# Nine expert units instead of ten: two experts' worth of places given to four in one of the units loaded ahead

## The chip, the core and the metric

The kernel runs on one core of one Trainium2 chip. The metric is device time in microseconds of one execution, taken as the median of a few runs. TensorE multiplies, VectorE, ScalarE and GpSimd (POOL in the profile) do the rest, SyncE (SP) issues loads, and 16 DMA engines move the bytes. The profile calls TensorE PE, VectorE DVE and ScalarE ACT.

## The reference

The reference is one decoder block for 256 tokens of width 1024 in float32. A forgetting attention and a gated delta rule run side by side and are merged. Then comes a mixture of 32 experts, each of which has three weights of 1 MiB (1024x256, 1024x256, 256x1024). Last come a per-layer input embedding, gated by a 1024x1024 weight, and a normalization. The change lies in the mixture, which is this:

```python
gl = t @ w_group + b_group                       # 4 groups
g_sel = argmax(gl);  p_sel = softmax(gl)[g_sel]
el = (t @ w_router + b_router)[group g_sel]      # 8 experts of the group
top_p, top_i = top_k(softmax(el), 2);  top_p /= sum(top_p)
gate = one_hot(g_sel) x (p_sel * top_p at top_i) # 256 x 32, two entries a token
for e in range(32):
    hid = silu(t @ w_gate[e]) * (t @ w_up[e])
    out = out + gate[:, e:e+1] * (hid @ w_down[e])
...
x = x + sigmoid(rmsnorm(x) @ w_ple_gate) * (p @ w_ple_proj)
```

Each token chooses two of 32 experts, so an expert gets 16 tokens on average. With the reference's inputs, the experts 0 to 5 get 17, 31, 12, 12, 14 and 21 tokens. The others, in descending order, get 36, 23, 23, 21, 21, 20, 18, 17, 17, 17, 16, 16, 16, 15, 15, 15, 13, 13, 11, 11, 11, 11, 9, 8, 6 and 6.

## The kernel before

The first 250 us are the two mixing branches, the output projection and the routing. While they run, SP already loads the weights of the experts 0 to 5 (`NSTAY = 6`), which are taken whatever the routing is. The other 26 are ordered by their number of tokens on the chip (`order_experts`). POOL then loads their weights with indirect transfers, whose row indices come from that order. "Expert 6" and so on below mean places in this order.

A **unit** is a set of experts that are computed together, and `UNITS` lists them. A unit always has 128 rows. A unit of two experts gives each 64 places for tokens, one of four gives each 32. Before the change there are ten units: four pairs (experts 0 to 7) and six fours (8 to 31). The last units are the **late** ones, from `UE = NU - 3` on, thus units 7, 8 and 9. Their experts have few tokens, so that only the first 16 of each 32 places (`FEW`) count. If an expert has more tokens than places, the flag that `order_experts` computes is set. A branch (`crowded`, `overflow`) then runs a loop over all experts and windows of 64 tokens. When the flag is not set, every engine jumps over it.

What happens for unit i:

- `group(i // 2)` gathers the token features of two units at once: VectorE writes 0/1 choices into the tile `G` (`one_hot`), TensorE multiplies the tokens (`xx`, high and low parts) by them into `ga`, and ScalarE copies the result into `XT`. `XT` has three halves that rotate, and `half(i)` says which half of a group a unit uses.
- `gate_up` multiplies `XT` by each expert's gate and up weights. Each expert of the unit writes its own 64 or 32 rows of the result tiles `gate` and `up`.
- `silu` and `hidden` form the hidden values, turn them (`hidT`) and multiply by the down weights into `dn` (and `ga` for the second half of a late unit).
- `parts` spreads an early unit's result over the tokens: `C` is the turned choice, and the products go into the four tiles `sum`. A late unit's result goes through `late_parts`, `late_spread` (into the finished rows) and `z_late`. The latter multiplies its turned rows by the final gate weight and spreads the product into the final gate's sums.

The final gate's product for the tokens as the early units leave them is made ahead, in `z_early`: 64 products of 128x512 with `w_ple_gate`, which start after the gate of the first late unit (`after("gate", UE + 1)`). `early_features` makes their operand once all early units are in. `last_down`, `z_last` and what they call finish the last unit in three pieces.

The weights go through a ring of places of 1 MiB: 20 in the expert stage, one more late (`xx`). `experts(u)` queues for each unit its gate weights, then the up weights, then the down weights. The down weights of the late units and of the one ahead of them go in halves or quarters. The extra embedding's weight `wpp` is queued ahead of expert 6. The four tiles of the final gate weight, `wpg`, are queued ahead of the gate weights of the unit that `WPG = (7, "g")` names. `Ring.pump` issues the next load as soon as a place is free, strictly in the order of the queue. Eight loads can be under way on POOL's queue, since each waits for the one eight issues earlier.

A planner (`Plan`) with rough costs merges the generators into one fixed order of instructions for each engine when the kernel is built. At run time each engine takes its instructions in that order. Every operation goes through one helper, so that the profile shows most of them at line 77, and tiles tell more than lines. An f32 product is two records in the profile and one row in the order.

Of the kernel before, what the change touches and what calls it, by code (L numbers as in the profile page):

```python
# [10 lines left out]
AF = mybir.ActivationFunctionType  # L11
OP = mybir.AluOpType
# [7 lines left out]
E = 32  # L20
CAP = 64


NSTAY, NWIDE = 6, 8
UNITS = [list(range(e, e + 2)) for e in range(0, NWIDE, 2)] + [list(range(e, e + 4)) for e in range(NWIDE, E, 4)]
NU = len(UNITS)

WPG = (7, "g")

UE, UL = NU - 3, NU - 1  # L30

FEW = 16
FIRST = UNITS[UE - 1][0]
# [64 lines left out]
class Plan:  # L98
# [25 lines left out]
    def after(self, name, n=1):  # L124
        return lambda: 0.0 if n <= 0 else self.told[name][n - 1] if len(self.told.get(name, ())) >= n else None
# [166 lines left out]
def hybrid_block(tc, x, p_t, w_in, w_o_fox, w_o_delta, w_out, w_gate, w_up, w_down, w_ple_gate,  # L292
                 w_ple_proj, g_final, keep_in, mix_in, out, dbg=None):
    nc = tc.nc
    plan = Plan(nc)
    V, S, P, G = plan.V, plan.S, plan.P, plan.G
# [80 lines left out]
    def K(name):  # L377
        a, b = KEEP[name]
        return kp[:, a:b]

    ident = K("ident")
    ones = keep.tile([128, 128], F32, name="ones")
# [846 lines left out]
    def last_tile():  # L1229
        for n in range(2):  # L1230
            yield after("sq1", n + 1)
            turned(1, n)
            yield
        logits(1, 0)
        yield
        yield after("sel")
        rank(0)
        logits(1, 1)
        yield
        yield from ffn_norm(1)  # L1240
        yield
        yield after("parts", 2)

        d = td[:, 0, :].rearrange("p (e s) -> p e s", s=CAP)
        for e in range(4):
            S.activation(d[:, e, :], K("slots"), AF.Square, scale=-1.0, bias=rk[:, 0, e:e + 1])
        S.activation(g0[:, 0].rearrange("p a (e s) -> p (a e) s", s=CAP), d, AF.Relu, scale=-1.0, bias=ones[:, 0:1])
        pr[1] = ps_t("mm")
        P.matmul(pr[1][:, 0:E], ones, sel[:, 0, :], start=True, stop=False)
        busy(6)  # L1250
        for k in range(4):
            gather(0, k)
        yield from route(1)
        rank(1)
        for k in range(4, 8):
            gather(0, k)
        busy(0)
        places(1)
        yield
# [71 lines left out]
    def half(i):  # L1331

        return (i % 2) ^ (i // 2 % 3 == 1)
# [64 lines left out]
    def order_experts():  # L1398
        yield after("sel", 2)
        pt = ps_t("dn")  # L1400
        for t in range(2):
            P.matmul(pt[0:32, 0:32], ones[:, 0:32], sel[:, t], start=t == 0, stop=t == 1)
        for t in range(2):
            P.matmul(pt[0:32, 32:33], sel[:, t], ones[:, 0:1], start=t == 0, stop=t == 1)
        yield
        keys, key, at = so[:, 0:32], so[:, 32:33], so[:, 33:34]
        V.scalar_tensor_tensor(key, pt[0:32, 32:33], 64.0, K("base")[0:32, 32:33], op0=OP.mult, op1=OP.add)
        V.scalar_tensor_tensor(keys, pt[0:32, 0:32], 64.0, K("base")[0:32, 0:32], op0=OP.mult, op1=OP.add)
        V.tensor_scalar(keys, keys, key, None, op0=OP.is_gt)
        V.tensor_reduce(at, keys, axis=AX.X, op=OP.add)  # L1410
        V.tensor_scalar(perm, K("places")[0:32, 0:32], at, None, op0=OP.is_equal)
        yield
        pt = ps_t("dn")
        P.matmul(pt[:, 0:32], K("places")[0:32, 32:33].to_broadcast([32, 128]), perm, start=True, stop=True)
        yield
        V.tensor_scalar(idx, pt[:, 0:32], K("places")[:, 33:34], None, op0=OP.add)
        tell("idx")
        V.tensor_scalar(rowf, pt[:, E - late:E], K("places")[:, 33:34], None, op0=OP.add)
        ring.index, ring.pieces = idx, idp
        ring.pump()  # L1420
        yield
        yield after("gate")
        yield from permute(rk, rkp, K("w_rt")[0:32, 0:256])
        tell("rkp")
        for (a, b), ix in idp.items():
            V.tensor_scalar(ix, rowf, 4.0 / (b - a), float(a // (b - a)), op0=OP.mult, op1=OP.add)
        yield after("weights")
        r = mo.tile([128, 2, 128], F32, name="hidT").rearrange("p k s -> p (k s)")[0:32]
        yield from permute(gr[:, :, :, 1], grp[:, :, :, 1], r)
        V.tensor_copy(grp[:, :, :, 0], gr[:, :, :, 0])  # L1430
        tell("grp")

        V.tensor_scalar(so[:, 34:35], at, NWIDE - 0.5, 32.0, op0=OP.is_lt, op1=OP.mult)
        V.tensor_scalar(so[:, 35:36], at, UNITS[UE][0] - 0.5, float(FEW - 32), op0=OP.is_gt, op1=OP.mult)
        V.tensor_tensor(so[:, 34:35], so[:, 34:35], so[:, 35:36], op=OP.add)
        yield
        pt = ps_t("sum00")
        P.matmul(pt[:, 0:32], so[:, 34:35].to_broadcast([32, 128]), ident[0:32, 0:32], start=True, stop=True)
        yield
        for t in range(2):  # L1440
            V.scalar_tensor_tensor(rko[:, t], rk[:, t], -32.0, pt[:, 0:32], op0=OP.add, op1=OP.subtract)
        V.tensor_reduce(big[:, 0:1], rko.rearrange("p t e -> p (t e)"), axis=AX.X, op=OP.max)
        yield
        pt = ps_t("sum00")
        P.transpose(pt[0:1, 0:128], big[:, 0:1], ident)
        yield
        V.tensor_reduce(big[0:1, 1:2], pt[0:1, 0:128], axis=AX.X, op=OP.max)
        V.tensor_scalar(flag, big[0:1, 1:2], 1.0, None, op0=OP.is_ge)
        tell("flag")
        yield  # L1450
# [16 lines left out]

    def group(i):

        yield after("rows", 2 * i - 2)  # L1470
        yield after("group", i - 1)
        yield after("G", i)
        g = mo.tile([128, 2, 2, 128], F32R, name="G") if i % 2 else g0
        X = XT[:, (slice(0, 2), slice(0, 3, 2), slice(1, 3))[i % 3]]
        wt = mo.tile([128, 2, 2], F32, name="wt", bufs=2)
        QD[i] = (g, wt)
        if i:
            yield after("rkp")
        for t in range(2) if i else (1,):
            yield after("rk", t + 1)  # L1480
            ranks = rkp if i else rk
            if half(2 * i) or 2 * i < UE <= 2 * i + 1:
                for a in range(2):
                    h = half(2 * i + a)
                    one_hot(g[:, t, h:h + 1], ranks[:, t], UNITS[2 * i + a])
            else:
                one_hot(g[:, t], ranks[:, t], UNITS[2 * i] + UNITS[2 * i + 1])
        tell("G")
        yield after("parts", 2)
        yield after("group", i)  # L1490
        yield after("gu", max(0, 2 * i - 1))
        for k in range(8):
            if i:
                yield turn()
                pt = ps_t("ga")[:, 0:256]
                n = 0
                for t in range(2):
                    for part in (xH, xL):
                        P.matmul(pt, part[:, t, k, :], g[:, t].rearrange("p a s -> p (a s)"), start=n == 0, stop=n == 3)
                        n += 1  # L1500
                plan.add(features_of(i, k, X, pt))
            else:
                gather(1, k)
                if k % 2:
                    for kk in (k - 1, k):
                        plan.add(features_of(i, kk, X, xb[kk // 2][:, kk % 2 * 256:kk % 2 * 256 + 256]))
                if k < 7:
                    continue
            yield
        yield after("grp" if i else "weights")  # L1510
        yield turn()

        pt = ps_t("ga")
        for a in range(2):
            u = UNITS[2 * i + half(2 * i + a)]
            m = 128 // len(u)
            for t in range(2):
                for o, e in enumerate(u):
                    P.matmul(pt[o * m:(o + 1) * m, 2 * a:2 * a + 2], g[:, t, a, o * m:(o + 1) * m].bitcast(F32), (grp if i else gr)[:, t, e, :],
                             start=t == 0, stop=t == 1, skip_group_check=True)  # L1520
        yield
        V.tensor_copy(wt.rearrange("p a b -> p (a b)"), pt[:, 0:4])
        tell("wt")
        tell("ga")
        tell("group")
        yield

    def features_of(i, k, X, pt):
        pt = pt.rearrange("p (a s) -> p a s", a=2)
        if True:  # L1530
            S.activation(X[:, :, k], pt, AF.Copy, scale=K("g_ffn")[:, k:k + 1])
        else:
            V.tensor_scalar(X[:, :, k], pt, K("g_ffn")[:, k:k + 1], None, op0=OP.mult)
        tell(f"X{i}")
        if i:
            tell("ga")
        yield
# [598 lines left out]
        nc.sync.dma_start(out[t * 128:(t + 1) * 128, 0:512], th)  # L2136
        yield

    for i in range(NU // 2):
        plan.add(group(i))  # L2140
    plan.add(add_x2())
    plan.add(order_experts())
# [95 lines left out]
```

## Time and profile before

| | |
|---|---|
| median of 3 runs | 536.14 us (535.42 to 536.36) |
| the profiled execution | 535.39 us, of which its span is 533.4 us |
| mean granted TensorE clock | 0.969 |
| TensorE busy | 499.9 us, 94% of the span |
| VectorE, ScalarE, GpSimd busy | 229.7, 210.4 and 133.9 us |
| moved by DMA | 141.25 MB, 265 GB/s over the span |
| loads issued by POOL (software_dynamic) | 86.01 MB |
| gate products of units 7, 8 and 9 start at | 411.49, 447.96 and 483.38 us |

The span runs from the first to the last instruction, and all times inside it count from its start. A busy TensorE need not be TensorE at its peak. A row of the chain of work says when a piece starts, how long it is, and on which engine and tile. A row of POOL's timeline shows an issue of a load, and in brackets how long POOL stood idle before it and what ended that.

### The profile page before, as it was taken

The page shows a single profiled execution, that of the slowest core. Times are in us where ns is not written, and L with a number is a line of the kernel's source. Part 1 is how long each engine was busy: PE and PEld are TensorE (multiplying, and loading weights), DVE is VectorE, ACT ScalarE, POOL GpSimd, SP SyncE. Part 2 cuts the span into 40 slices and gives each one's busy share as a digit, 9 for nine tenths or more (in the row PEclk, how much of TensorE's full clock was granted, in tenths as well). Part 3 has the DMA queues.
Part 4 walks back from the last instruction along what each step waited for, and adds up shares of the span by engine and source line. Part 5 has one row for each costly group of instructions (what it writes and reads, how often), then busy time and mean ns, then how long its engine had stood idle before and what let it go on. Part 6 is the DMA issues. An engine that isn't in the chain of part 4 may idle for free. (4 is left out here: it accounts for less than half of the span.)

```text
span 533.4 us, 10476 instructions
## 1 busy us (share of the span) xinstructions
PE 499.9 (94%) x4375; PEld 351.0 (66%) x4375; DVE 229.7 (43%) x543; ACT 210.4 (39%) x475; POOL 133.9 (25%) x160
## 2 busy tenths in 40 slices
PE   7999999999999999979999999968986999989993
PEld 7999998899999999868555554423543444433441
DVE  3888689764655659584311111100123011012246
ACT  5576845566734545344231221203244011021144
POOL 5000551200000000061233324316444226425000
PEclk9999999999999999998999999979996999998997
DMA  8845533223098569875979999998999996985002
GB/s 343 347 159 167 192 119 115 67 89 131 7 402 303 170 225 423 314 289 188 358 278 384 367 378 340 373 396 308 412 421 416 421 412 227 421 349 201 1 1 79
DMA packets 25605, 141.25 MB, mean 265 GB/s; under 512 B 2625, under 2 KB 2897, under 8 KB 12626
## 3 DMA queue, kind: packets, MB, share of 16 engines
q0 software_dynamic: 14752, 86.01, 41.3%
q1 hardware_dynamic: 10658, 54.01, 27.0%
q8 instruction: 36, 0.59, 0.4%
q10 hardware_dynamic: 144, 0.52, 0.2%
q14 instruction: 15, 0.12, 0.1%
HBM read 139.46 MB, written 1.05 MB: 263 GB/s over the span
## 5 line engine op out<-in xcount | busy, mean ns | idle before, releaser
L77 PE MATMUL mm<-hH,ra 128*128 128x256 f32 x688 | 127.1, 284 | 0.0
L77 PEld LDWEIGHTS mm<-hH,ra 128*128 128x128 f32 x688 | 105.6, 188 | 1.5 <-issue 0.3
L77 PE MATMUL mm<-hL,ra 128*128 128x256 f32 x344 | 83.8, 281 | 0.5 <-DVE hL L77 0.5
L77 PEld LDWEIGHTS mm<-hL,ra 128*128 128x128 f32 x344 | 64.8, 188 | 1.4 <-DVE hL L77 0.7
L77 DVE TENSOR_TENSOR ra<-ra,ra 128x1024 fp32r<-128x1024 f32 x41 | 50.3, 1231 | 18.2 <-ACT ra L77 18.2
L77 ACT CAST ra<-ra 128x1024 fp32r<-128x1024 f32 x41 | 42.9, 1053 | 27.1 <-PE mm L77 23.2
L77 DVE TENSOR_TENSOR yL<-dn,yH 128x512 fp32r<-128x512 f32 x16 | 11.1, 692 | 71.8 <-ACT yH L77 71.8
L77 ACT ACTIVATE XT<-ga,kp 128x256 f32<-128x256 f32 x32 | 15.1, 473 | 55.3 <-PE ga L77 55.3
L77 POOL CAST xx<-xt 128x1024 fp32r<-128x1024 f32 (+1 forms) x2 | 3.3, 1648 | 126.5 <-ACT td L77 123.8
L77 PE MATMUL gate<-ra,XT 128*32 128x256 f32 (+1 forms) x224 | 34.0, 402 | 0.0
L77 PE MATMUL up<-ra,XT 128*32 128x256 f32 (+1 forms) x240 | 33.0, 393 | 0.0
L77 PE MATMUL ga<-G,xx 128*128 128x256 f32 x128 | 23.0, 303 | 7.7 <-PEq L1710 5.1
L77 PE MATMUL gate<-rb,XT 128*32 128x256 f32 (+1 forms) x176 | 30.2, 397 | 0.0
L77 PEld LDWEIGHTS ga<-G,xx 128*128 128x128 f32 x128 | 18.2, 193 | 16.6 <-issue 10.1
L77 DVE SCALAR_TENSOR_TENSOR kp<-th,wt,up 128x256 f32<-128x256 f32 x10 | 4.8, 480 | 52.8 <-PE up L77 52.8
L77 PE MATMUL dn<-ra,hidT 128*32 128x512 f32 (+2 forms) x88 | 23.1, 578 | 0.3 <-DVE rc L77 0.3
L77 PE MATMUL sum<-ra,xx 128*128 128x512 f32 x48 | 22.9, 599 | 0.0
L77 PEld LDWEIGHTS up<-ra,XT 128*32 128x32 f32 (+1 forms) x240 | 14.5, 120 | 11.2 <-issue 5.5
L77 PEld LDWEIGHTS gate<-ra,XT 128*32 128x32 f32 (+1 forms) x224 | 15.0, 124 | 10.2 <-issue 6.1
L77 ACT COPY hidT<-ga 128x256 f32<-128x256 f32 x10 | 3.7, 372 | 40.9 <-PE ga L77 40.9
L77 ACT CAST yH<-dn 128x512 fp32r<-128x512 f32 x16 | 9.3, 583 | 24.1 <-PE dn L77 14.1
L77 PE MATMUL gate<-rc,XT 128*32 128x256 f32 (+1 forms) x64 | 18.0, 416 | 0.0
(477 smaller groups left out, 1097.5 us busy)
## 6 DMA issues: line engine op xcount, KB each, us to landing
ra<-in_w_in SPq DMA_DIRECT2D x19, 1024.0 KB, 5.1
ra<-in_w_gate SPq DMA_DIRECT2D x4, 1024.0 KB, 4.9
ra<-in_w_out SPq DMA_DIRECT2D x3, 1024.0 KB, 4.8
ra<-in_w_up SPq DMA_DIRECT2D x3, 1024.0 KB, 5.0
ra<-in_w_ple_gate POOLq DMA_DIRECT2D x3, 1024.0 KB, 11.1
ra<-in_w_o_fox SPq DMA_DIRECT2D x2, 1024.0 KB, 5.6
rq<-in_w_in SPq DMA_DIRECT2D x2, 1024.0 KB, 10.6
rq<-in_w_down SPq DMA_DIRECT2D x2, 1024.0 KB, 8.1
```

The source lines that it names most:

```text
L77: return f(*a, **k)
```

## The change

Experts 2 to 5 become one unit of four with 32 places each, where they were two pairs with 64. The units are now [0, 1], [2, 3, 4, 5], [6, 7] and six fours. There are nine of them. `UE` becomes `NU - 2`, so units 7 and 8 are late, with the experts 24 to 31; before, the late ones held the experts 20 to 31. The experts 20 to 23 become an early unit with 32 places. `WPG` still names unit 7, which now begins with expert 24 instead of 20, so the final gate weight is loaded behind the experts 20 to 23. The rest adapts code to this: the choices of the first group are made for a pair and a four, the flag's limits take 32 places for the experts 2 to 5, and the last group has a single unit.

```diff
-NSTAY, NWIDE = 6, 8
-UNITS = [list(range(e, e + 2)) for e in range(0, NWIDE, 2)] + [list(range(e, e + 4)) for e in range(NWIDE, E, 4)]
+NSTAY = 6
+UNITS = [[0, 1], [2, 3, 4, 5], [6, 7]] + [list(range(e, e + 4)) for e in range(8, E, 4)]
 NU = len(UNITS)
 WPG = (7, "g")
-UE, UL = NU - 3, NU - 1
+UE, UL = NU - 2, NU - 1
...
-        d = td[:, 0, :].rearrange("p (e s) -> p e s", s=CAP)
-        for e in range(4):
-            S.activation(d[:, e, :], K("slots"), AF.Square, scale=-1.0, bias=rk[:, 0, e:e + 1])
+        d = td[:, 0, :]
+        for i in range(2):
+            m = 128 // len(UNITS[i])
+            for o, e in enumerate(UNITS[i]):
+                S.activation(d[:, 128 * i + o * m:128 * i + (o + 1) * m], K("slots")[:, 0:m], AF.Square, scale=-1.0,
+                             bias=rk[:, 0, e:e + 1])
...
-        V.tensor_scalar(so[:, 34:35], at, NWIDE - 0.5, 32.0, op0=OP.is_lt, op1=OP.mult)
+        x = so[:, 0:1]
+        V.tensor_scalar(x, at, -3.5, None, op0=OP.add)
+        V.tensor_tensor(x, x, x, op=OP.mult)
+        V.tensor_scalar(x, x, 4.0, None, op0=OP.is_gt)
+        V.tensor_scalar(so[:, 34:35], at, 7.5, 32.0, op0=OP.is_lt, op1=OP.mult)
+        V.tensor_tensor(so[:, 34:35], so[:, 34:35], x, op=OP.mult)
...
+        us = range(2 * i, min(2 * i + 2, NU))
+        hs = slice(half(2 * i), half(2 * i) + 1) if len(us) == 1 else slice(0, 2)
...
-                        P.matmul(pt, part[:, t, k, :], g[:, t].rearrange("p a s -> p (a s)"), start=n == 0, stop=n == 3)
+                        P.matmul(pt[:, 0:128 * len(us)], part[:, t, k, :], g[:, t, hs].rearrange("p a s -> p (a s)"),
+                                 start=n == 0, stop=n == 3)
...
-    for i in range(NU // 2):
+    for i in range((NU + 1) // 2):
         plan.add(group(i))
```

How it moves instructions is shown at three places. In the rows of the order, numbers behind a tile's name tell its versions apart, and xN is a run of like instructions.

TensorE at the gate of unit 1, before: two experts' weights (`rb_2741`, `rb_2743`) take turns, 64 rows of the result each.

```order
L77 MATMUL sum_3336<-kp,gr 32x128 x2
L77 MATMUL gate<-rb_2741,XT 64x256
L77 MATMUL gate<-rb_2743,XT 64x256
L77 MATMUL gate<-rb_2741,XT 64x256
L77 MATMUL gate<-rb_2743,XT 64x256
L77 MATMUL ga<-G,xx_2735 128x256
```

After: four experts' weights take turns, 32 rows each.

```order
L77 MATMUL sum_3335<-perm,hidT 128x32 x2
L77 MATMUL gate<-rb_2741,XT 32x256
L77 MATMUL gate<-rb_2743,XT 32x256
L77 MATMUL gate<-rb_2745,XT 32x256
L77 MATMUL gate<-ra_2852,XT 32x256
L77 MATMUL gate<-rb_2741,XT 32x256
L77 MATMUL gate<-rb_2743,XT 32x256
L77 MATMUL gate<-rb_2745,XT 32x256
L77 MATMUL gate<-ra_2852,XT 32x256
L77 MATMUL ga<-G,xx_2735 128x256
```

The unit has twice the instructions, with half the rows each.

POOL's queue at the final gate weight, before: its tiles are queued behind the down weights of unit 6 (experts 16 to 19) and ahead of the gate weights of unit 7 (experts 20 to 23).

```order
L209 DMA ra_4613<-in_w_down,idp_3193 128x1024
L209 DMA rb_4615<-in_w_down,idp_3193 128x1024
L202 DMA rc_4638<-in_w_ple_gate 128x2x1024
L202 DMA ra_4685<-in_w_ple_gate 128x2x1024
L202 DMA ra_4687<-in_w_ple_gate 128x2x1024
L202 DMA ra_4689<-in_w_ple_gate 128x2x1024
L209 DMA ra_4691<-in_w_gate,idx 128x2048
```

After: the down weights ahead of it are those of the experts 20 to 23, and the gate weights behind it those of 24 to 27.

```order
L209 DMA rb_4788<-in_w_down,idp_3195 128x1024
L209 DMA rc_4790<-in_w_down,idp_3195 128x1024
L202 DMA ra_4796<-in_w_ple_gate 128x2x1024
L202 DMA ra_4826<-in_w_ple_gate 128x2x1024
L202 DMA rb_4828<-in_w_ple_gate 128x2x1024
L202 DMA rb_4830<-in_w_ple_gate 128x2x1024
L209 DMA ra_4832<-in_w_gate,idx 128x2048
```

The final gate weight has moved twelve loads back in the order of loading, and still stands at unit 7.

TensorE behind the late product of unit 7, before: the first half of unit 8's down products (second turn of its four experts), the spread of unit 7's late product (`sum<-yH,G`), and the second half of unit 8's down products, which goes to `ga`. The rest of unit 8 and the gate of unit 9 follow.

```order
L77 MATMUL dn<-rq_5085,hidT 32x512
L77 MATMUL dn<-rq_5087,hidT 32x512
L77 MATMUL dn<-rc_5136,hidT 32x512
L77 MATMUL dn<-ra_5138,hidT 32x512
L77 MATMUL sum_5111<-yH,G 128x512
L77 MATMUL sum_5111<-yL,G 128x512
L77 MATMUL sum_5220<-yH,G 128x512
L77 MATMUL sum_5220<-yL,G 128x512
L77 MATMUL ga<-rq_5085,hidT 32x512
L77 MATMUL ga<-rq_5087,hidT 32x512
L77 MATMUL ga<-rc_5136,hidT 32x512
L77 MATMUL ga<-ra_5138,hidT 32x512
```

After: the down products at this place are the last unit's, and its smaller pieces (256 columns) follow the spread at once.

```order
L77 MATMUL dn<-rq_5194,hidT 32x512
L77 MATMUL dn<-ra_5196,hidT 32x512
L77 MATMUL dn<-ra_5245,hidT 32x512
L77 MATMUL dn<-rc_5247,hidT 32x512
L77 MATMUL sum_5220<-yH,G 128x512
L77 MATMUL sum_5220<-yL,G 128x512
L77 MATMUL sum_5321<-yH,G 128x512
L77 MATMUL sum_5321<-yL,G 128x512
L77 MATMUL dn<-rq_5194,hidT 32x256
L77 MATMUL dn<-ra_5196,hidT 32x256
L77 MATMUL dn<-ra_5245,hidT 32x256
L77 MATMUL dn<-rc_5247,hidT 32x256
```

A whole late unit is gone from between the two.

More of the change, by code (lines that the diff above doesn't have):

```diff
@@ L1242, in last_tile @@
         yield after("parts", 2)
-        d = td[:, 0, :].rearrange("p (e s) -> p e s", s=CAP)
-        for e in range(4):
-            S.activation(d[:, e, :], K("slots"), AF.Square, scale=-1.0, bias=rk[:, 0, e:e + 1])
-        S.activation(g0[:, 0].rearrange("p a (e s) -> p (a e) s", s=CAP), d, AF.Relu, scale=-1.0, bias=ones[:, 0:1])
+        d = td[:, 0, :]
[4 more added lines that the diff above has]
+                             bias=rk[:, 0, e:e + 1])
+        S.activation(g0[:, 0].rearrange("p a s -> p (a s)"), d, AF.Relu, scale=-1.0, bias=ones[:, 0:1])
         pr[1] = ps_t("mm")
@@ L1481, in group @@
             ranks = rkp if i else rk
[L1482 to L1485, printed above, removed]
-            else:
-                one_hot(g[:, t], ranks[:, t], UNITS[2 * i] + UNITS[2 * i + 1])
+            if i in (1, 3) or half(2 * i) or len(us) == 1:
+                for u in us:
+                    h = half(u)
+                    one_hot(g[:, t, h:h + 1], ranks[:, t], UNITS[u])
+            elif i:
+                one_hot(g[:, t], ranks[:, t], UNITS[2 * i] + UNITS[2 * i + 1])
+            else:
+                for u in us:
+                    one_hot(g[:, t, u:u + 1], ranks[:, t], UNITS[u])
         tell("G")
@@ L1498, in group @@
                     for part in (xH, xL):
-                        P.matmul(pt, part[:, t, k, :], g[:, t].rearrange("p a s -> p (a s)"), start=n == 0, stop=n == 3)
+                        P.matmul(pt[:, 0:128 * len(us)], part[:, t, k, :], g[:, t, hs].rearrange("p a s -> p (a s)"),
+                                 start=n == 0, stop=n == 3)
                         n += 1
-                plan.add(features_of(i, k, X, pt))
+                plan.add(features_of(i, k, X[:, hs], pt[:, 0:128 * len(us)]))
             else:
@@ L1513, in group @@
         pt = ps_t("ga")
-        for a in range(2):
-            u = UNITS[2 * i + half(2 * i + a)]
+        for a in range(2)[hs]:
+            u = UNITS[2 * i + (half(2 * i + a) if len(us) > 1 else 0)]
             m = 128 // len(u)
@@ L1521, in group @@
         yield
-        V.tensor_copy(wt.rearrange("p a b -> p (a b)"), pt[:, 0:4])
+        V.tensor_copy(wt[:, hs].rearrange("p a b -> p (a b)"), pt[:, 2 * hs.start:2 * hs.stop])
         tell("wt")
@@ L1528, in features_of @@
     def features_of(i, k, X, pt):
-        pt = pt.rearrange("p (a s) -> p a s", a=2)
+        pt = pt.rearrange("p (a s) -> p a s", s=128)
         if True:
```

## The prediction

> **What bounds the kernel now.** I read the slices of the span first, then busy time by stage, then POOL's own rows (POOL issues the expert weights), then the chain of work that ended last.
>
> ```profile
> PE   7999999999999999979999999968986999989993
> ...
> DMA  8845533223098569875979999998999996985002
> GB/s 343 347 159 167 192 119 115 67 89 131 7 402 303 170 225 423 314 289 188 358 278 384 367 378 340 373 396 308 412 421 416 421 412 227 421 349 201 1 1 79
> ```
>
> A slice is 13.3 us. From slice 19 on TensorE and the loads are both nearly full: in the expert stage there are two bounds side by side. The stages say which of them yields:
>
> ```profile
> core 0: us, PE busy (x) PEld busy (x) DVE busy (x) ACT busy (x) POOL busy (x), PEclk, DMA share, GB/s
> 258.70:292.50 33.80, 33.80 (x236) 18.49 (x236) 6.32 (x21) 8.34 (x18) 11.20 (x12) 1.00 0.87 331
> 292.50:411.50 119.00, 104.27 (x888) 51.84 (x888) 19.40 (x43) 32.50 (x64) 47.46 (x52) 0.94 0.97 379
> 411.50:448.00 36.50, 36.50 (x228) 16.15 (x232) 4.35 (x7) 4.58 (x9) 14.24 (x15) 0.95 0.92 365
> 448.00:483.40 35.40, 33.72 (x240) 13.54 (x242) 4.76 (x9) 4.55 (x9) 15.22 (x17) 0.95 0.91 359
> 483.40:533.40 50.00, 40.72 (x298) 17.76 (x298) 20.27 (x57) 16.84 (x41) 4.54 (x5) 0.94 0.16 58
> 268.30:409.40 141.10, 127.05 (x1050) 64.03 (x1048) 22.99 (x50) 37.38 (x75) 55.58 (x60) 0.96 0.95 373
> 370.00:440.00 70.00, 62.50 (x528) 30.98 (x524) 12.98 (x25) 18.50 (x34) 29.36 (x32) 0.93 1.01 413
> ```
>
> Seventy microseconds at 413 GB/s show what the loads can sustain; the mean from 268.3 to 409.4 is 373. TensorE has no gap in 258.7 to 292.5 and in 411.5 to 448.0, and there the loads are slower. POOL's rows tell why:
>
> ```profile
> 268.26 0.94 POOL L209 DMA_INDIRECT rb<-in_w_down,idx  x1 [7.42 <-PE gate L77]
> 313.34 0.94 POOL L209 DMA_INDIRECT ra<-in_w_up,idx  x1 [0.30 <-issue]
> 340.28 0.94 POOL L209 DMA_INDIRECT ra<-in_w_gate,idx  x1 [8.14 <-PE gate L77]
> 401.94 0.93 POOL L209 DMA_INDIRECT rc<-in_w_down,idp  x1 [1.04 <-DMA ra<-in_w_up,idx]
> 409.48 0.93 POOL L209 DMA_INDIRECT ra<-in_w_down,idp  x1 [1.48 <-DMA rq<-in_w_up,idx]
> 441.52 0.94 POOL L209 DMA_INDIRECT rc<-in_w_down,idp  x1 [8.34 <-PE ga L77]
> 488.22 0.95 POOL L209 DMA_INDIRECT rq<-in_w_down,idp  x1 [0.30 <-issue]
> ```
>
> Three times POOL stands 7 to 8 us until TensorE has finished a unit and freed its ring places: TensorE paces the loads. Only around 402 to 409 does POOL wait for loads in flight, eight issues back; those four landings (one a row, first and last shown) are 2.5 us apart, 1 MiB each, the 413 GB/s again. TensorE is the bound, the loads run a little ahead of it, and the ring ties them.
>
> The end of the chain, with the units counted from 0 (7, 8, 9 are the late ones):
>
> ```profile
> 411.49 5.28 PE gate L77 x64
> 416.78 7.92 PE sum L77 x18
> 424.70 3.59 PE up L77 x64
> ...
> 447.96 1.00 PE gate L77 x16
> ...
> 471.88 1.85 PE dn L77 x16
> ...
> 483.38 1.00 PE gate L77 x16
> ...
> 495.32 3.59 PE up L77 x64
> ...
> 501.36 1.90 PE dn L77 x16
> ...
> 528.15 0.75 DVE rb L77
> ```
>
> 411.49, 447.96 and 483.38 are the gates of units 7, 8 and 9; 471.88 and 501.36 the first down product of units 8 and 9. Nearly every piece is TensorE's. The last load is issued at 488.22, and the span goes on for 45 us.
>
> **The change, part by part.**
>
> One unit less. What a unit costs TensorE does not hang on its width:
>
> ```profile
> 258.66 1.08 PE L77 MATMUL gate<-rb,XT 128*64 128x256 f32 x8
> 326.15 1.07 PE L77 MATMUL up<-ra,XT 128*32 128x256 f32 x16
> ```
>
> Eight records of a pair (64 columns each) take 1.08 us, sixteen of a four (32 columns) 1.07: two or four experts run side by side. So the new unit 1 (experts 2 to 5) costs what unit 1 cost with experts 2 and 3. The new units 0 to 6 take, index for index, the TensorE time of the old units 0 to 6, and the old list of work between their gates (gathers, spreads, the extra input embedding) stays, in another order at a few places. By TensorE alone the gate of unit 7 stays at 411.5. Behind it the order of unit 7 and of the early part of the final gate product is the old one up to the last products of unit 7; then, where the old list has the rest of unit 8 and the front of unit 9, the new one goes straight to the last unit's down products. What drops out of the chain is the stretch from 471.88 to 501.36, 29.5 us. From the gate of unit 7 to the end there remain (471.9 - 411.5) + (533.4 - 501.4) = 60.4 + 32.0 = 92.4 us. TensorE alone would end at 411.5 + 92.4 = 503.9.
>
> The loads. The gate of unit 7 now needs experts 24 to 27, which were unit 8; the four tiles of the final gate weight stand ahead of them in both orders. Counting tiles of 1 MiB in the order of loading, the one issued at 268.26 is the 25th; the old unit 7 needed 69, the new one 81. From the 25th to the 81st are 57 tiles and a quarter MiB of the extra input: 60.0 MB. At 413 GB/s from the end of that issue (269.2) this takes 145.4 us, to 414.6. In the first microseconds the queue must fill again: nothing, or 3 us, as slow as the first slices behind 268 were in before; I take 2.5. The gate of unit 7 comes at 417.1, which is 5.6 us behind TensorE's own 411.5, and the loads set it. The rate I take is 413 and not 373, because what held the old one was the wait for places, and these now come free earlier: the end of unit 1's gate frees four places where it freed two, its up and down the same, so where POOL issued the 42nd tile at 313.34 it may then issue the 52nd, some eight or more ahead of landing, and it stays ahead to 411. If that cover goes, 373 is the other end. Behind unit 7's gate the loads have slack: 20 tiles, 50.8 us at 413, end at 468, and the last down begins at 417.1 + 60.4 = 477.5.
>
> Unit 8's extras. One late unit less also means one turned set of features, one late product with the gate weight and one spread of it less; all of that lies in the 29.5 us.
>
> The final gate weight's 64 early products (the sums at 416.78 and behind) keep their place behind unit 7's gate, so nothing new covers or uncovers them; that they now meet two late units instead of three is in the 92.4.
>
> Small additions, ahead of the first unit:
>
> ```profile
> 239.95 1.06 ACT L77 ACTIVATE td<-kp,rk 128x64 f32<-128x64 f32 x4 [1.80 <-DVE rs_ffn L77]
> 240.91 2.91 PE L77 MATMUL gate<-ones 128*128 128x128 f32 x12
> 245.42 0.46 DVE L77 TENSOR_TENSOR G<-kp,rk 128x256 fp32r<-128x256 f32 x1
> 261.32 0.19 DVE L77 TENSOR_SCALAR so<-so 32x1 f32<-32x1 f32 x2
> 266.85 0.14 DVE L77 TENSOR_SCALAR flag<-ovf 1x1 int32<-1x1 f32 x1
> 337.98 0.90 DVE L77 TENSOR_TENSOR G<-kp 128x128 fp32r<-128x128 f32 x4
> ```
>
> Two more activations at 0.27 (1.06 over four): 0.53 us, covered by the filler products that end at 243.8; without them 0.53. The first unit's choice in two halves: 2 x 0.225 against 0.46, nothing; at worst 0.46. Four tiny VectorE steps at 0.1 ahead of the flag: 0.4 us, and at 266.85 the flag is ready long before the branch; nothing. The single last gather of 128 columns instead of 256 may give back up to 2 us; I take none.
>
> Sum: 417.1 + 92.4 = 509.5 of span, plus the 2.0 that the profiled execution has around it (535.4 against 533.4): 511.5 against 535.4, 23.9 less. The median of the runs, 536.14, lies 0.75 above the profiled execution, so the forecast is 512.2.
>
> **The rivals.**
>
> The loads keep the old pace. If 373 GB/s is what indirect loads give here and not what places allow, 60.0 MB take 160.9 us, the gate comes at 430.1, the end is 522.5 + 2.75 = 525.3. For it: even where the share is 0.97 the rate is only 379. Against it: 413 over 70 us, when POOL stood eight loads ahead.
>
> A cap. Indirect loads that run for long may settle at what the two late stages show, 365 and 359; at their middle, 362, the 60.0 MB take 165.7 us, the gate comes at 434.9, and 530.1 follows, next to no gain. The row of 413 over 70 us speaks against it. The Trainium skill, SBUF — State Buffer, Summary: rules for kernel authors, has a rule of this kind: it puts transfers between HBM and SBUF at about 358 GB/s, by which 531.9 would be my estimate; the 413 of this trace is above that figure.
>
> TensorE alone. Loads never late: 503.9 + 2.75 = 506.7.
>
> Slower. The ring runs dry: places now come free in fours, POOL issues strictly in order, and a wait like the 8 us at 340.28 recurs at each gate of units 3 to 7. It decides from the point where the gate of unit 7 comes later than 441.0, 29.5 us behind the old one, so below 60.0 MB / 171.8 us = 349 GB/s; at the 331 of the row 258.7 to 292.5 the gate comes at 450.5 and 545.6 follows. Against it: the wait at 268.26 falls where TensorE has 20 tiles in hand, and a unit that stands until its loads arrive gives its places back at once.
>
> The change isn't free of overflow: an expert among 2 to 5 with over 32 tokens sets the flag, and the loop over all experts and windows reloads 4 x 96 MiB, about 975 us at 413 GB/s. By the reference with its inputs these four get 12, 12, 14 and 21.
>
> **How the numbers follow.** The forecast holds with 0.66; its own range is 507 (420 GB/s, no fill) to 517 (400 GB/s, 3 us). The old pace: 0.17, spread over 518 to 530. TensorE alone: 0.08. The cap: 0.03. The dry ring: 0.05, of which 0.01 ends within 0.2% of before, about what a measurement here tells from no change. Overflow: 0.01. Faster 0.66 + 0.17 + 0.08 + 0.03 = 0.94, same 0.01, slower 0.05. The range 504 to 524 takes the forecast, TensorE alone and under half of the old pace: 0.8.
>
> **What would show it.** Right: 410 GB/s or more from about 275 to 465; unit 7's gate near 417, waiting for its weights; 60 us from there to the last unit's first down and 32 to the end; POOL waiting for earlier loads and not for TensorE. Wrong: a rate near 370 with POOL waiting for gates; the gate of unit 7 behind 430; new gaps of TensorE behind it.

## The result, and the profile after

The nine-unit kernel takes 513.82 us (median of 4 runs, 513.53 to 514.43). The kernel before, beside it, takes 536.25 us (535.42 to 536.90). The ratio is 0.9584, with a 95% interval from 0.9567 to 0.9601. It is 22.4 us faster; the forecast was 512.2 us.

The profiled execution after takes 514.43 us, its span 512.7, at a mean granted clock of 0.963. First the slices of its span (12.8 us each): busy tenths of TensorE and of the DMA engines, and what they moved.

```profile
PE   7999999999999999998999998858978879999993
...
DMA  8953452222259558976678999999999999994002
GB/s 340 368 175 133 161 201 86 86 84 83 83 228 402 192 175 321 421 287 203 246 318 325 424 424 419 416 417 419 422 419 409 417 419 410 424 412 169 1 0 82
```

From slice 22 to slice 35 (the first slice is 0) the loads run at 409 to 424 GB/s without a dip. Before, the same row went up and down between 227 and 421 over this part. TensorE had four slices of 6 or 8 tenths among slices 24 to 32 before, and now has eight of 5 to 8 tenths. The stretches of the span say the same in one row each (columns as in the prediction: length, busy time of each engine with its count of records, granted clock, DMA share, GB/s):

```profile
257.58:420.05 162.47, 141.71 (x1289) 68.98 (x1287) 26.85 (x68) 40.95 (x84) 65.04 (x70) 0.95 0.99 403
280.00:460.00 180.00, 159.47 (x1349) 74.94 (x1352) 25.71 (x52) 39.32 (x79) 76.47 (x83) 0.94 1.02 418
420.05:480.58 60.53, 60.53 (x412) 26.30 (x416) 6.63 (x11) 6.01 (x12) 23.89 (x25) 0.97 0.79 320
480.58:512.70 32.12, 22.78 (x129) 10.33 (x128) 16.09 (x50) 14.04 (x35) 0.00 (x0) 0.94 0.09 33
```

The chain that ended last, in the rows that answer to those of before:

```profile
418.93 1.12 PE ga L77 x4
420.05 5.42 PE gate L77 x64
425.47 7.92 PE sum L77 x18
433.39 3.59 PE up L77 x64
...
456.66 1.00 PE gate L77 x16
...
480.58 1.90 PE dn L77 x16
...
507.38 0.75 DVE rq L77
```

420.05 is the gate of unit 7, 456.66 that of unit 8 (now the last), and 480.58 the first down product of the last unit. From the gate of unit 7 to that product there are 60.53 us without a gap of TensorE, and 32.12 from there to the end. The forecast had 60.4 and 32.0. Nearly all that is off lies ahead of 420.05, where the forecast had 417.1. The row above the gate is one of the last early features (TensorE turning them in `ga`), and it ends where the gate starts, so this profile shows no wait for a weight there. POOL's rows show how close the loads were, with the time that the load issued at 400.12 took to land (smallest, median and largest, of this one load):

```profile
371.95 0.94 POOL L209 DMA_INDIRECT ra<-in_w_up,idx  x1 [10.84 <-PE gate L77]
...
400.12 0.93 POOL L209 DMA_INDIRECT rb<-in_w_gate,idx  x1 [1.83 <-DMA rc<-in_w_down,idp]
...
417.80 1.12 POOL L209 DMA_INDIRECT rq<-in_w_down,idp  x1 [1.55 <-DMA ra<-in_w_gate,idx]
420.28 0.93 POOL L209 DMA_INDIRECT rb<-in_w_down,idp  x1 [1.36 <-PE ga L77]
```

```profile
DMA to landing us min/median/max: 19.4/19.4/19.4
```

At 417.80 the third of unit 7's four gate weights had landed. The fourth, issued at 400.12, landed 19.4 us later, at 419.5. In this profile TensorE's list and the loads arrive at the gate within half a microsecond, TensorE last. The experiments had to tell which of them sets it.

### The profile page after: what moved, and what is told of

It is laid out like the page before. It is cut to its first block, busy times and chain, and to the rows that moved or that the text cites. A ratio compares the mean times of both kernels' runs of the same rounds, so it can differ in the third digit from the quotient of the medians.

```text
span 512.7 us, 10318 instructions
## 1 busy us (share of the span) xinstructions
PE 475.7 (93%) x4313; PEld 340.4 (66%) x4313; DVE 223.1 (44%) x534; ACT 204.1 (40%) x465; POOL 131.2 (26%) x156
## 5 line engine op out<-in xcount | busy, mean ns | idle before, releaser
L77 PE MATMUL gate<-ra,XT 128*32 128x256 f32 (+1 forms) x208 | 37.8, 405 | 0.0
L77 PE MATMUL up<-ra,XT 128*32 128x256 f32 (+1 forms) x304 | 35.2, 383 | 0.0
L77 ACT ACTIVATE XT<-ga,kp 128x256 f32<-128x256 f32 (+1 forms) x32 | 14.3, 447 | 45.0 <-PE ga L77 44.8
L77 PE MATMUL dn<-rq,hidT 128*32 128x512 f32 (+2 forms) x64 | 28.1, 624 | 0.3 <-DVE rq L77 0.3
L77 PE MATMUL ga<-G,xx 128*128 128x256 f32 (+1 forms) x128 | 23.4, 307 | 4.1 <-ACT XT L77 2.6
L77 PE MATMUL dn<-rb,hidT 128*32 128x512 f32 (+1 forms) x68 | 26.4, 649 | 0.0
L77 PE MATMUL gate<-rq,XT 128*32 128x256 f32 x96 | 25.6, 406 | 0.0
L77 PE MATMUL sum<-rb,xx 128*128 128x512 f32 x68 | 24.5, 490 | 0.0
L77 PEld LDWEIGHTS up<-ra,XT 128*32 128x32 f32 (+1 forms) x304 | 16.9, 115 | 10.4 <-issue 3.3
L77 PE MATMUL gate<-rb,XT 128*32 128x256 f32 x144 | 21.8, 399 | 0.0
L77 ACT CAST yH<-dn 128x512 fp32r<-128x512 f32 x15 | 8.8, 583 | 29.5 <-PE dn L77 17.1
```

Source lines behind the costliest of these rows:

```text
L77: return f(*a, **k)
```

## Experiments

A first group of four ran on one chip. The kernel before took 536.59 us there (534.89 to 538.13, 7 runs), and every ratio is to that.

**Loads earlier.** The final gate weight goes behind the gate weights of unit 7.

```diff
-WPG = (7, "g")
+WPG = (7, "u")
```

> The four tiles of the final gate weight are queued behind unit 7's gate weights instead of ahead of them, so those gate weights land four tiles, 4 x 2.5 = 10 us, earlier. The loads set unit 7's gate (the forecast's step): the gate moves from 420.0 to TensorE's own 411.5 to 415 and the time falls from 513.8 to 505 to 509. TensorE's own list also ends at 420 (a tie): the gate stays at 419 to 421 and the time at 513 to 515. Rival, a new wait: the final gate's early products lack their weight, a gap of TensorE opens behind unit 7's gate, and the time is above 516.

Measured: 518.73 us, ratio 0.9668 (0.9645 to 0.9692), 4.9 us above the nine-unit kernel. POOL's row that waits for the fourth gate weight, and then the chain:

```profile
409.30 0.94 POOL L209 DMA_INDIRECT ra<-in_w_up,idx  x1 [1.57 <-DMA rb<-in_w_gate,idx]
```

```profile
419.17 0.69 PE ga L77 x2
419.86 5.90 PE gate L77 x64
425.76 19.15 PE sum L77 x44
444.91 3.59 PE up L77 x64
...
483.84 1.90 PE dn L77 x16
```

The weights were there at 409, and the gate still started at 419.86, straight behind the early features. So TensorE's own list reaches the gate at 420 with the loads ten microseconds ahead of it, as the tie expects. The time is that of the rival, but the early products do not wait for their weight. The planner put 44 of them in one piece ahead of `up` (19.15 us, where it was 18 in 7.92). From the gate to the last unit's first down TensorE now takes 63.98 us instead of 60.53, and the rest of the span 33.66 instead of 32.12. That is 5.0 us, which is the loss. TensorE's idle time makes up 2.8 of them (it waits for `th`, `kp` and `rq` of the last unit, 3.1 us in all instead of 0.3): the early products are missing as filler there. The other 2.2 are longer busy time.

**TensorE earlier.** The branch over the overflow loop goes.

```diff
-        slots = overflow()
+        slots = ring.take(F32)[1], ring.take(F32R)[1]
```

> The branch over the overflow loop is left out on every engine, with the loop, so an expert with too many tokens would not be served; the reference's inputs have none. The rest of the order stands. TensorE stood 5.1 us at this branch and ran at a lower granted clock around it. TensorE's own list sets unit 7's gate: the gate moves from 420.0 to 412 to 415 and the time falls to 506 to 509. The loads set it, alone or in a tie: the last of unit 7's gate weights still lands near 420, the gate stays at 418.5 to 420.5, now with a wait of TensorE for it, and the time is 512.5 to 514.5.

Measured: 513.46 us, ratio 0.9598 (0.9560 to 0.9637): no gain that can be told. TensorE's rows at unit 7's gate, and the fourth weight's load as the chain shows it:

```profile
410.65 1.11 PE L77 MATMUL ga<-kp,rq 128*128 128x128 f32 x4 [0.68 <-ACT xx L77]
411.69 0.64 PE L77 MATMUL gate<-ra,XT 128*32 128x256 f32 x1
...
414.88 1.06 PE L77 MATMUL gate<-ra,XT 128*32 128x256 f32 x2 [2.11 <-DMA ra<-in_w_gate,idx]
417.19 0.64 PE L77 MATMUL gate<-rb,XT 128*32 128x256 f32 x1 [1.26 <-DMA rb<-in_w_gate,idx]
```

```profile
396.99 20.16 DMA rb<-in_w_gate,idx
```

Here is the forecast's picture: TensorE arrives at 411.69, and stands until the third and the fourth weight land, the fourth at 417.15. That both lie within 0.2 us of the forecast (411.5 and 417.1) is luck, since the forecast is of a kernel with the branch, and there they came at 420.05 and 419.5. The fourth weight also came earlier than expected (418.5 to 420.5); the time is the one expected if the loads set the gate. So the loads have an end of their own at 417 to 420.

**Both.** The two edits above together.

> Both edits: unit 7's gate weights ahead of the final gate weight, and no branch over the overflow loop (left out with the loop). A tie of loads and TensorE at 420: only now does the gate move, to 412 to 415, and the time falls to 506 to 509, though neither edit alone gave more than 1.5 us. One of them alone sets the gate: the time is that of the edit that takes it away, within 1 us.

Measured: 510.83 us, ratio 0.9530 (0.9509 to 0.9551).

```profile
412.00 5.61 PE gate L77 x64
417.61 19.15 PE sum L77 x44
...
475.69 1.90 PE dn L77 x16
```

Only with both edits does the whole gate move, to 412.00; without the branch alone its last weights held it to 417.19. This is the tie. The time fell by 3.0 us and not by the 5 to 8 expected, because this kernel also pays the price of the queue, here 4.5 us (63.69 + 33.51 instead of 60.53 + 32.12).

**Half of the change.** The kernel before with ten units and all its pairs, but two late units instead of three. (The last line of the edit keeps `C2` in the tile that it had.)

```diff
-UE, UL = NU - 3, NU - 1
+UE, UL = NU - 2, NU - 1
-WPG = (7, "g")
+WPG = (8, "g")
-        PR["C2", i] = QD[UE // 2][0]...
+        PR["C2", i] = QD[(UE - 1) // 2][0]...
```

> The kernel before with its ten units and four pairs, but two late units instead of three: experts 20 to 23 become an early unit, and the final gate weight stands ahead of experts 24 to 27. This is one part of the change alone. If the gain is the unit (the forecast's 29.5 us of list that drops out): a late unit took 35.4 us between its gates in the kernel before and the four units ahead of it 29.8 us each, so 536.2 falls by up to 5.6, to 530 to 534. If the gain is that only two late units remain (a late unit's turn, product and spread, and the wait for its own result): 515 to 522. If a late unit costs no more than an early one: 535 to 538.

Measured: 522.76 us, ratio 0.9755 (0.9734 to 0.9776), 13.8 us less than before: just above the 515 to 522 expected if the gain is that only two late units remain. The gate of unit 8, here the first late one, and the first down of the last unit:

```profile
429.13 3.59 PE gate L77 x64
...
487.84 1.90 PE dn L77 x16
```

The 29.8 us between two gates were the wrong measure of an early unit. As an early unit, the experts 20 to 23 move the first late gate from 411.49 to 429.13, which is 17.6 us. Behind that gate, 121.9 us (533.4 - 411.5) become 90.8 (519.9 - 429.1), which is 31.1 less. So over half of the 22.4 us come from two late units instead of three, and some 9 from the four that takes the place of two pairs. The split holds for this order of the two halves; the four with three late units was not run.

The same run says what the four does for the loads. This is 280 to 380 us in this kernel, then in the nine-unit kernel:

```profile
280.00:380.00 100.00, 92.65 (x733) 44.11 (x733) 12.38 (x26) 21.73 (x45) 34.19 (x37) 0.97 0.95 373
```

```profile
280.00:380.00 100.00, 88.80 (x791) 40.68 (x790) 10.42 (x24) 21.26 (x44) 37.06 (x40) 0.93 1.01 420
```

With the pairs, loads run at 373 GB/s; with a four in their place, at 420. The number of late units is the same in both, so it isn't that. Nor is it the chip: the kernel without the branch, a nine-unit kernel on the same chip as this run, has 421 in this stretch.

**The planner's price of a load.** The planner takes loads for 360 GB/s. A second group, on another chip, tried 415, alone and with other queues.

```diff
-        self.free["D"] = max(self.free["D"], since) + nbytes / 360e3
+        self.free["D"] = max(self.free["D"], since) + nbytes / self.RATE   # 360e3 up to here
...
+        plan.RATE = 415e3                    # in order_experts, ahead of its ring.pump()
```

> The nine-unit kernel with one number of the planner changed: expert loads are priced at 415 GB/s (as measured) instead of 360. Nothing is computed otherwise; only the order of TensorE's list changes, so that the gates of units 3 to 6 stand earlier, among the gathers and spreads. Theory A: TensorE's own list reached unit 7's gate 8.5 us later than the list of before because the planner took the loads for slower than they are. Then TensorE arrives at 412 to 415, the loads set the gate at 417 to 418, and the time falls to 510.5 to 512.5. Theory B: the 8.5 us are the branch and a lower granted clock, which this order has too: the gate stays at 419 to 421, the time at 513 to 515.

> The planner's price at 415 GB/s, and the final gate weight queued behind unit 7's gate weights. The two limits of unit 7's gate, TensorE's list and the loads, are both moved with nothing left out. Theory A: the gate starts at 408 to 413, partly among the last early features; from there to the last unit's first down 63 to 64 us as in the earlier run with this queue (its early products stand in one piece there), so 507 to 511. Theory B: the gate stays near 420 and the time is 516 to 520, as in that run.

The third has the same price, and the final gate weight in two halves:

```diff
-            if nm == WPG[1] and u is UNITS[WPG[0]]:
-                for k in range(4):
+            if nm in WPG[1] and u is UNITS[WPG[0]]:      # WPG = (7, "gu")
+                for k in (range(2) if nm == "g" else range(2, 4)):
```

> The planner's price at 415 GB/s, and two of the four tiles of the final gate weight ahead of unit 7's gate weights, two behind. The gate's loads land 5 us earlier than now, at 412 to 415, and the early products need their second half of the weight only later. Theory A: gate at 412 to 416, 60.5 to 62 us from there to the last first down, 32 to the end: 507 to 511. Theory B (TensorE's list sets 420 whatever the price): 513 to 516.

> The ten-unit kernel before, with the planner's price at 415 GB/s instead of 360. There the loads ran at 373 GB/s up to unit 7's gate, held by places, near the planner's price. If the wrong price hurts only where the loads run at 413 or more: 534 to 538. If the price costs the kernel before as much as the new one: 526 to 531.

On this chip the kernel before took 554.90 us (550.33 to 557.05), and no absolute number of these expectations can hold. Measured, in this order: price alone 533.88, ratio 0.9643 (0.9568 to 0.9718); with the later final gate weight 532.53, 0.9614 (0.9541 to 0.9686); with the split 526.33, 0.9515 (0.9431 to 0.9599); and for the kernel before with the price 553.69 (548.45 to 558.89), whose spread is wider than its distance from 554.90. All three intervals hold the 0.9584 that the unchanged nine-unit kernel had in the result; it was not run on this chip. The group settles nothing about theory A.

**Once more, beside the unchanged kernel.** A third group ran on a third chip, with the nine-unit kernel among them.

> The nine-unit kernel as it is, as the mark for the three that follow on the same chip: 513 to 515, 0.958 of the kernel before, unit 7's gate at 419 to 421.

> Once more the planner's price of 415 GB/s instead of 360, the only edit; in the run before TensorE had stretches without instructions that no other run shows. Theory A (the price spaces the gates and costs TensorE's list up to 8.5 us ahead of unit 7's gate): the loads then set the gate at 417 to 418, and the time is 1 to 3 us under the unchanged kernel. Theory B (the 8.5 us are the branch, the hops through ScalarE and VectorE and the granted clock, whatever the order): within 1 us of the unchanged kernel, or slower by what the new order happens to cost.

> Once more the price of 415 GB/s with two tiles of the final gate weight behind unit 7's gate weights. Theory A: both limits of the gate are moved, it starts at 411 to 415, and the time is 4 to 8 us under the unchanged kernel, 506 to 510. Theory B: the gate stays at 419 to 421 and the time is within 2 us of the unchanged kernel.

> The split of the final gate weight alone, with the planner's price at 360. The gate's loads land 5 us earlier, TensorE's list up to the gate is unchanged. Either theory, with the tie at 420: the gate stays at 419 to 421, and the time is that of the unchanged kernel or up to 3 us more, since the early products follow in another order. If the loads alone set the gate: 509 to 511.

The kernel before took 557.54 us there (555.89 to 560.36, 11 runs).

| kernel | us | ratio to before | 95% | gate of unit 7 |
|---|---|---|---|---|
| nine units, unchanged | 543.10 | 0.9742 | 0.9709 to 0.9775 | 442.63 |
| price 415 | 536.19 | 0.9626 | 0.9590 to 0.9662 | 437.67 |
| final gate weight split | 537.64 | 0.9637 | 0.9609 to 0.9664 | 437.06 |
| both | 529.97 | 0.9512 | 0.9467 to 0.9557 | 432.96 |

The expected times were missed here too, the mark's own among them: on this chip the change is worth 14.4 us, not 22.4. The expected differences were missed as well: under the unchanged kernel by 6.9 us (price; 1 to 3 by theory A), 5.5 (split; none by either) and 13.1 (both; 4 to 8 by theory A). Between the four kernels the order is clear but for price and split, which lie close. Either edit gains 1.0 to 1.3%, both gain 2.4% (529.97 / 543.10 = 0.976). The version with both has the lowest ratio of all kernels run that keep the branch, 0.951 on two chips. It was not run on a chip where the kernel before takes 536 us, so whether it gains there is open.

Nor do these runs confirm theory A. In all four TensorE's list runs into the gate without a wait for a weight, as at 420.05 in the profile of the result. The split alone also brought the gate forward by 5.6 us, though the order of TensorE's list ahead of it is unchanged and the expectation was no move. Why is open. Up to unit 7's gate the unchanged kernel is both busy for longer on this chip (149.07 us from 260.00 to 442.63, at a granted clock of 0.91, against 141.71 from 257.58 to 420.05 at 0.95) and idle for longer (33.6 against 20.8). Idle time that the profile of the result does not have stands in its waits (engine, tile, what was waited for: us, times, longest), first two of TensorE's, then ScalarE's:

```profile
PE gate L77 <- issue: 1.9, 3, 0.8
PE dn L77 <- issue: 1.4, 1, 1.4
```

```profile
ACT XT L77 <- remote: 13.7, 3, 6.1
ACT yH L77 <- remote: 5.9, 1, 5.9
ACT yH L77 <- issue: 5.2, 1, 5.2
```

Engines stand for nothing that the profile can name ("issue"), or for another core or an unknown queue ("remote"). In the profile of the same kernel with 512.7 us of span these tiles have no such rows. The loads suffer with them. This is the DMA share and rate from 350 to 400 us in 40 slices of 1.25 us, and POOL's row behind the second of the two holes:

```profile
DMA  9999999999998100899999995000069989999998
GB/s 413 413 419 419 426 419 433 419 406 419 419 419 341 79 0 0 184 406 419 406 426 426 413 439 236 20 0 0 0 118 426 374 334 400 393 413 419 400 400 341
```

```profile
384.94 0.94 POOL L209 DMA_INDIRECT ra<-in_w_up,idx  x1 [11.85 <-PE gate L77]
```

POOL waited 11.85 us for the gate of unit 5, and the queue ran dry for several microseconds. In the profile of the result it waited almost as long at the same place (10.84 at 371.95), and the loads in flight covered it. The first hole stands behind a wait of 9.53 us, where it was 6.89. So the dry ring, a rival of the forecast, does occur once other stalls are added. What holds the engines up on these chips is not shown.

## Why the prediction was right

**Sign, size, mechanism.** The gain comes, as forecast, from one unit less in the chain, with loads fast enough to let it shrink: 23.9 us forecast against its own profiled execution, 21.0 measured (535.39 to 514.43) and 22.4 between the medians. The time lies in the likeliest case's own range (507 to 517).

**The chain behind unit 7's gate** was right to 0.2 us: 60.53 and 32.12 against 60.4 and 32.0.

**The rate of the loads** was right, and so was its reason. 418 GB/s over 180 us answers the forecast's 413 against the old pace of 373 and the cap of 362. The half of the change shows that the four is the cause. At the place that the forecast named, around 313 us, POOL had waited for TensorE; it now waits for a load in flight. First a row of before, then one of after:

```profile
312.10 0.94 POOL L209 DMA_INDIRECT ra<-in_w_gate,idx  x1 [4.75 <-PE up L77]
```

```profile
313.11 0.94 POOL L209 DMA_INDIRECT ra<-in_w_down,idx  x1 [1.55 <-DMA rb<-in_w_gate,idx]
```

On the cap the Trainium skill has a second rule, in Perfetto Trace Analysis, Engine Utilization (Roofline): 358 GB/s is a core's share when both cores of a pair load, and a core alone is bounded by its DMA engines at about 435. The 418 of this trace, of a kernel on one core, fits this rule, and not the flat 358 that the forecast names beside its rival of the cap.

**The gate of unit 7** is the term that was mis-sized: 420.05 instead of 417.1. The step said that TensorE alone stays at 411.5 and that the loads set the gate. Its loads part was 2.4 us short (419.5): the 25th tile was issued 0.9 us later than before (269.19), and from there the weights took 149.4 us instead of 147.9. TensorE's own part failed: its list came 8.6 us later than the old one, and last. In the terms of half of the change, the four takes the gate from 429.13 to 420.05, which is 9.1 us, where the forecast counted a whole early unit. Here are the rows from the end of unit 0's gate to the gate of unit 7, in the kernel before; the one of after stands above (257.58:420.05):

```profile
256.34:411.49 155.15, 140.42 (x1139) 71.33 (x1137) 27.36 (x72) 41.68 (x84) 58.68 (x64) 0.96 0.95 368
```

The stretch of after starts 1.2 us later, has 1.3 us more of busy time, and idles 20.8 instead of 14.7 us. The later start need not be the change's: the nine-unit kernel without the branch, which is the same up to there, starts this stretch at 256.31. The idle time is what the forecast missed: it had put "another order at a few places" at nothing. Those places are in the waits of TensorE from 290 us to the gate, after:

```profile
PE ga L77 <- PEq L1724: 5.1, 1, 5.1
PE ga L77 <- ACT XT L77: 3.6, 7, 0.6
PE dn L77 <- DVE yL L77: 2.8, 2, 1.4
PE ga L77 <- DVE xx L77: 2.0, 2, 1.2
```

The 5.1 us at the skipped branch were there before too, and so was most of the waits for `XT` (3.4) and `xx` (1.6). The down products that wait for `yL` (2.8) were not; both halves of a unit's down now stand so close that the second waits until the first has left its tile. The rest is spread over short hops. Nothing here gives a reason for such a list and the loads to come out at the same 420. That the miss is only 2.95 us is luck: TensorE's list, 8.6 us late, came just behind loads that the forecast had put 5.6 us behind TensorE's old arrival.

**POOL's waits** were right for a part of the stage only. The forecast had POOL waiting for earlier loads and not for TensorE. Rows like the 10.84 us at 371.95 still wait for TensorE; they cost the loads nothing here, because the loads in flight last as long: 422 and 419 GB/s in the two slices from 359 to 385.

**What the forecast did not see** is the split of the 29.5 us. It named the late unit's extras (turned features, product with the final gate weight, spread) and left them in one sum. Half of the change, run alone, prices them: the experts 20 to 23 take 31.1 us as a late unit and 17.6 as an early one. Without it a reader would credit the gain to the merged pairs.

The median came out 1.6 us above the forecast: the span 3.2 more, the time around it 0.3 less (514.43 against 512.7), and the median 0.6 below the profiled execution where 0.75 above was taken.

## What to carry to other kernels

Price a unit of work by the stage that it leaves, and not by the mean of its kind: the same four experts cost 17.6 us as an early unit and 31.1 as a late one. Where two chains meet at one point, lengthen or shorten each alone and then both; a run with one edit that gains nothing does not say that the edit is idle. And a new order of an engine's list has a price of its own even where the work is the same (6 us more of idle time here), so look at the stalls ahead of the meeting point before counting the whole gain. Whether the planner's price of a load is the cause is not shown: a price of 415 gained 6.9 us on one chip, but not in the way that was expected.

## What the hardware showed beyond expectation

Jumping over a loop costs TensorE 5.1 us of standing still (5.06 before, 5.08 after, 4.0 to 6.4 in the other runs that have the branch), though the loop never runs. What leaving it out is worth shows in the stretch from the last `up` product ahead of the branch to unit 7's gate, in the nine-unit kernel, without the branch, and with both edits:

```profile
338.70:420.05 81.35, 63.70 (x552) 31.34 (x548) 12.70 (x25) 23.11 (x45) 33.15 (x36) 0.92 1.02 417
```

```profile
335.96:411.69 75.73, 62.58 (x548) 30.87 (x540) 12.69 (x25) 23.14 (x45) 31.72 (x34) 0.95 1.02 418
```

```profile
338.37:412.00 73.63, 60.73 (x552) 30.17 (x548) 10.90 (x22) 19.29 (x41) 30.23 (x33) 0.98 1.01 417
```

Without the branch the stretch is 5.6 and 7.7 us shorter, more than the stall. TensorE's idle time falls by 4.5 and 4.8 us; the rest is busy time, at a higher granted clock (0.95 and 0.98 instead of 0.92). The run without the branch was also 2.7 us ahead at the start of the stretch; that part of its 8.4 us (411.69 against 420.05) cannot come from the branch. The Trainium skill, Advanced Engine Details and Errata, Control Flow Timing, gives a compare-and-branch about 108 ns. The standing still in this trace, 5.1 us, is far longer, and for this place the trace decides.

The loads of one core held 418 GB/s for 180 us. And the same kernel pair differed by 22.4 us on one chip and by 14.4 us on another, where the kernel before takes 557.5 us instead of 536.3.
